# Both halves of the activations side by side, and one 512-column product for the upper weights

## The chip, the cores and the metric

The kernel runs on one core of a Trainium2 chip. The metric is the device time of one execution, in microseconds (us): from the runs below, the median of three. The core has five engines that take their instructions from queues of their own and wait for each other by semaphores: TensorE (PE in the profile, with the loads of its stationary operand as PEld), VectorE (DVE), ScalarE (ACT), GpSimd (POOL) and SyncE (SP), which here only starts transfers.

## What is computed

The reference runs two transformer layers' worth of blocks over 256 tokens of 1024 features, in float32. Cut to what matters here:

```
h    = rms_norm(x)                       # [256, 1024]
proj = h @ w_in                          # 10 blocks of 1024 columns: q, k, v, conv (3), q_m, gates (3)
o    = diff_attention(q, k, v)           # 8 heads, two softmaxes each
conv = gate_b * causal_conv(gate_c * x_c)
x    = x + (g0*(o @ w_attn_o) + g1*(conv @ w_conv_o) + g2*(mem_attn @ w_mem_o)) @ w_o
x    = x + square(relu(h2 @ w_mlp_in)) @ w_mlp_out            # 1024 -> 4096 -> 1024
# second block: mod = silu(c) @ ada_w (adaLN), grouped-query attention + MLP, gated MLP over tokens + MLP
```

Nearly all the work is matrix products of 256 tokens with weights of 1024 rows or more; the weights are read once each.

## The kernel before

**Three products for one.** TensorE multiplies float32r operands, which hold fewer bits than float32. So each operand is split into an upper half, rounded to float32r, and a lower half, the rest. A product is then three: upper by upper, activation's lower by weight's upper, activation's upper by weight's lower, all added up in one PSUM bank. The class `Weights` loads 1 MB of weights at a time (`raw`, three buffers, line 64 on SP's queue) and splits it in two *halves*: the upper part by a cast on ACT (line 86), the lower part by a subtraction on DVE (line 87). It does this in the order of use, six halves ahead of TensorE, into a ring of seven. `W.get` takes the next half, `W.done` says that one is used up and issues the cast for the half six further on and the subtraction for the one before it.

**Three kinds of product loop.** `gemm_cols` (line 407) and `Rows` (505) keep 128 tokens stationary and stream 512 columns of weights through `mm3` (396 to 399). `gemm_feat` (491 to 503) is the other way round: a 128x128 block of weights is stationary and 256 tokens are streamed, so that the result has features on the partitions. One call makes 256 features: for `j` = 0 and 1, one half of weights each, 8 steps `k` with three matmuls of 256 columns (497, 498, 499). Both `j` write one bank `[2, 256]`, and the caller reads the bank when both are done. There are 84 calls: 12 in the gated convolution, 24 in the merging of the three branches, 12 in each of three MLPs, 12 in the gated MLP of the second block.

**Activations.** An activation operand (`hT`, `oT`, `omT`, `cvT`, `mgT`, `memh`, `act`) is a list of two tiles `[128, 8, 256]`, upper and lower. `split_to` (276 to 278) fills them: a cast on ACT, a subtraction on DVE.

**The order of work** is the program's order on each engine, written by hand. `tick()` (378) is called between halves: it runs what is due (`later`), one filler from a list, and now and then a step of the adaLN product (`ada_step`, 1002: ACT starts a transfer, DVE multiplies and adds). In the convolution the fillers are the eight heads of differential attention, four ticks a head and in a software pipeline: `dif_a` (860: scores on PE, mask and maxima on DVE, four exponentials on ACT), then `dif_ot` and `dif_b` (883: DVE mixes the two softmaxes), then `dif_o` and `dif_n`, then `dif_t` (896: PE transposes what `dif_b` wrote, line 900).

**Who reads the banks of gemm_feat.** Convolution (963 to 981): `xc` is copied by ACT; the second product is multiplied by it on DVE (970) and convolved there (974, 976); the third is multiplied on DVE (979) and split. Branches (1045): ACT's sigmoid, and DVE's product. MLP (1142 to 1146): `square` is a Relu and a Square on ACT (1118, 1120), then `split_to`; in each quarter of an MLP four calls are followed by eight halves of `Rows`. Gated MLP (1399): ACT's Gelu.

**PSUM.** Two rings of four banks: `ps_a` (products of most stages, and `dif_t` in the convolution) and `ps_x` (everything else, and `gemm_feat` in the MLPs and the gated MLP). A bank is taken again when its last reader is done.

Of the kernel before, what the change touches and what calls it, by code (L numbers as in the profile page):

```python
# [15 lines left out]
P = 128  # L16
# [6 lines left out]

class Weights:
    """The weights in the order of their use: 1 MB loads, each split in two halves into
    operands hi (rounded to float32r) and lo (the exact rest)."""
# [66 lines left out]
    def first(self, kind, key):  # L93
        """The index of the first half of a load."""
        return 2 * next(i for i, u in enumerate(self.plan) if u[:2] == (kind, key))
# [8 lines left out]
    def done(self, rest=True):  # L104
        """One more half is used up: go on with the loads and splits (lo only up to rest() if told so)."""
        self.used += 1
        self.pump()
        if rest:
            self.rest(self.KEEP)
# [3 lines left out]
def kernel(  # L113
# [28 lines left out]
    # ------------------------------------------------------------------ the weights' order  # L142
# [53 lines left out]
    # ------------------------------------------------------------------ loads at the start  # L196
# [12 lines left out]
    memh = [memin.tile([P, 8, 256], F32R, name=f"memh{i}") for i in range(2)]  # L209
# [50 lines left out]
    # ------------------------------------------------------------------ helpers  # L260
    def rsqrt(ss, inv, y, E=None):
        """y = 1/sqrt(ss*inv + EPS) by Newton's steps from the usual first guess."""
# [26 lines left out]
    def transposed(t, xn, gcol, bcol, dst):  # L289
        """A function that makes dst[hi, lo][:, :, tokens t] = (xn * g + b)^T, xn in two halves."""  # L290
# [38 lines left out]
    def norm(t, src, ssp, gcol, bcol, dst, E=None):  # L329
        """dst[hi, lo][:, :, tokens t] = (src over its root mean square * g + b)^T with g, b per feature;  # L330
        ssp: the sums of squares of src's halves. In three parts: this one, and two to be called later."""
# [32 lines left out]
    def later(n, f):  # L364
        """f runs n ticks on."""
        due.append((clock[0] + n, f))
# [40 lines left out]
    def gemm_cols(key, n0, act, evac, fill=1, acc=None, i0=0):  # L407
        """512 columns: act^T (tokens on partitions out) @ w; evac(the token tiles' psums)."""
# [13 lines left out]
    def gap():  # L422
        """A product that may run while TensorE would wait for operands."""
        if gaps:
            gaps.popleft()()

    def gemm_cols_skew(key, n0s, act, evacs, second, fill=1):
        """The first two of some chunks of columns: the first token tile runs six halves of weights
        ahead, while second() makes the operands of the other."""
# [36 lines left out]
    def gemm_cols_start(key, n0, act, evac, second, fill=1):  # L466
        """The first columns: two halves of weights for a token tile in turn; second() makes the operands
        of the other."""
# [22 lines left out]
    def gemm_feat(key, f0, act, p=ps_a, fill=1):  # L491
        """256 features: w^T @ act (features on partitions out), in one bank [2, 256 tokens]."""
        acc = bank(p).rearrange("p (j c) -> p j c", j=2)
        for j in range(2):
            wh, wl = W.get("B", (key, f0))
            for k in range(8):
                T.matmul(acc[:, j], wh[:, k, :], act[0][:, k, :], start=(k == 0), stop=False)  # L497
                T.matmul(acc[:, j], wh[:, k, :], act[1][:, k, :], start=False, stop=False)  # L498
                T.matmul(acc[:, j], wl[:, k, :], act[0][:, k, :], start=False, stop=(k == 7))  # L499
            W.done()  # L500
            if j == 0:
                tick(fill)
        return acc

    class Rows:
        """out [256, 1024] += act^T @ w by rows of w, in four banks."""
# [13 lines left out]
        def run(self, k0, acts, evac=None, fill=1):  # L520
            """acts: (act pair, index) of rows k0.. in order."""
# [45 lines left out]
    # ------------------------------------------------------------------ small vectors  # L567
# [10 lines left out]
    hT = [const.tile([P, 8, 256], F32R, name=f"hT{i}") for i in range(2)]  # L578
# [91 lines left out]
    # ------------------------------------------------------------------ memory attention  # L670
# [5 lines left out]
    def transpose4(src, dst, on_act=True, scale=None):  # L676
        """dst (a [P, 4, 128] view) = the four [128, 128] blocks of src [P, 512], transposed."""
# [60 lines left out]
    omT = [b1.tile([P, 8, 256], F32R, name=f"omT{i}") for i in range(2)]  # L738
# [10 lines left out]
    def softmax_a(ps, rs, p):  # L749
        """p [P, 2, 256] = exp(rs*(ps - max)) per row and half; returns the sums."""  # L750
# [15 lines left out]
    def transpose_p(p, dst, on_act=True):  # L766
        """p [P q, 2 t, 256 k] -> dst [P k, 2 kb, 256 q]"""
# [35 lines left out]
    def slots(nh, stages):  # L803
        """Software pipeline: per slot, groups of (lag, piece) become one filler each."""
# [6 lines left out]
    # ------------------------------------------------------------------ q, k, v of differential attention  # L811
# [48 lines left out]
    def dif_a(h):  # L860
        """Scores of a head's two components in a bank each: [P, 128 keys] and [P, 256 keys] of the two query tiles."""
# [75 lines left out]
    for n in range(2):  # L937
# [3 lines left out]
        if n == 0:  # L941
# [8 lines left out]
            oT = [oTp.tile([P, 8, 256], F32R, name=f"oT{i}") for i in range(2)]  # L950
# [5 lines left out]
    # ------------------------------------------------------------------ gated convolution  # L956
    convp = pool(right, "conv", side="right")
    cvT = [convp.tile([P, 8, 256], F32R, name=f"cvT{i}") for i in range(2)]
# [4 lines left out]
    for f in range(4):  # L963
        xc = tmp("kn", 2).rearrange("p (j c) -> p j c", j=2)
        ps = gemm_feat("in", XC + 256 * f, hT)
        S.copy(xc, ps)
        tick()
        ps = gemm_feat("in", GC + 256 * f, hT)
# [503 lines left out]
```

## Time and the profile before

| | |
|---|---|
| runs, us | 1336.23, 1336.67, 1340.35 (median 1336.67) |
| span of the profiled execution, us | 1335.7 |
| PE busy | 1315.5 us, 98% of the span, 7883 matmuls |
| PEld busy | 1141.9 us, 85% |
| DVE busy | 926.9 us, 69% |
| ACT busy | 731.2 us, 55% |
| POOL busy | 140.0 us, 10% |
| read from memory | 273 MB, 205 GB/s over the span |

The profile is of one execution, of which it gives the span from the first to the last instruction; no other time is given for that execution. Matmuls are pipelined: the busy time of one matmul (about 0.28 us for 256 columns) is longer than the distance to the start of the next, so what a matmul costs is read from starts in a timeline, and not from the busy column. A busy share is an average over stages.

### The profile page before, as it was taken

What the parts mean: (1) busy time and instruction counts of PE and PEld (TensorE: products, weight loads), DVE (VectorE), ACT (ScalarE), POOL (GpSimd) and SP (SyncE); (2) the same over time, 40 slices, a digit from 0 to 9 for tenths busy, and PEclk for the clock granted to TensorE, in tenths of its full rate; (3) what the DMA queues carried; (4) which work ended last, traced back from release to release, by engine and by line L of the source; (5) the groups of instructions that cost most, each with busy time, mean ns of one, the idle gap of its engine ahead of it and who ended that gap; (6) DMA issues with size and microseconds to landing.
All of it is one profiled execution on the core that took longest, in us unless ns stands there. A gap on an engine that the chain in (4) does not pass through costs nothing.

```text
span 1335.7 us, 20533 instructions
## 1 busy us (share of the span) xinstructions
PE 1315.5 (98%) x7883; PEld 1141.9 (85%) x7883; DVE 926.9 (69%) x1424; ACT 731.2 (55%) x1184; POOL 140.0 (10%) x375
## 2 busy tenths in 40 slices
PE   8899999999999999999899999999999999999998
PEld 6788789999998889987657889987789988799896
DVE  5555678755776778777776787676888877764453
ACT  6765665554444655445575755445646543674451
POOL 1522154500001000100400000000000000000000
PEclk8999999999999999999899999999999999999999
DMA  6572344456885788984313687894886765465650
GB/s 235 201 247 95 127 149 163 154 199 217 269 273 173 237 293 288 285 305 144 110 63 111 200 297 254 269 315 151 292 269 222 253 229 194 135 208 187 214 190 32
DMA packets 166959, 275.43 MB, mean 206 GB/s; under 512 B 8412, under 2 KB 95244, under 8 KB 166732
## 3 DMA queue, kind: packets, MB, share of 16 engines
q1 hardware_dynamic: 137260, 219.78, 48.7%
q10 hardware_dynamic: 27808, 50.41, 11.5%
q0 software_dynamic: 1792, 3.92, 1.1%
q8 instruction: 62, 1.02, 0.3%
q14 instruction: 37, 0.30, 0.1%
HBM read 273.04 MB, written 1.05 MB: 205 GB/s over the span
## 4 chain that ended last, share of the span: by engine, by line
PE 93%; DMA 2%; POOL 1%; DVE 1%; ACT 1%; issue 1%; SPq 0%; ACTq 0%; DVEq 0%; POOLq 0%
PE bank L397 15%; PE bank L399 15%; PE bank L398 15%; PE bank L497 12%; PE bank L499 12%; PE bank L498 12%; PE bank L447 2%; PE bank L1274 1%; PE bank L1254 1%; PE bank L1386 1%; PE bank L438 1%; PE bank L771 1%; PE bank L295 1%; PE bank L680 1%; PE bank L1034 1%
## 5 line engine op out<-in xcount | busy, mean ns | idle before, releaser
L86 ACT CAST whi<-raw 128x1024 fp32r<-128x1024 f32 x412 | 426.3, 1051 | 277.1 <-PE bank L399 79.7
L87 DVE TENSOR_TENSOR wlo<-raw,whi 128x1024 fp32r<-128x1024 f32 x412 | 496.3, 1220 | 90.7 <-ACT whi L86 89.6
L497 PE MATMUL bank<-hT,whi 128*128 128x256 f32 x1152 | 328.6, 285 | 0.0
L499 PE MATMUL bank<-hT,wlo 128*128 128x256 f32 x1152 | 324.8, 282 | 0.0
L498 PE MATMUL bank<-hT,whi 128*128 128x256 f32 x1152 | 324.5, 282 | 0.0
L497 PEld LDWEIGHTS bank<-hT,whi 128*128 128x128 f32 x1152 | 216.5, 188 | 1.9 <-issue 1.3
L498 PEld LDWEIGHTS bank<-hT,whi 128*128 128x128 f32 x1152 | 217.5, 189 | 0.6
L499 PEld LDWEIGHTS bank<-hT,wlo 128*128 128x128 f32 x1152 | 217.1, 188 | 0.0
L397 PE MATMUL bank<-whi,act 128*128 128x512 f32 x384 | 152.2, 396 | 0.0
L398 PE MATMUL bank<-wlo,act 128*128 128x512 f32 x384 | 151.7, 395 | 0.0
L399 PE MATMUL bank<-whi,act 128*128 128x512 f32 x384 | 151.6, 395 | 0.0
L397 PE MATMUL bank<-whi,hT 128*128 128x512 f32 x308 | 128.2, 416 | 0.8 <-ACT hT L321 0.8
L399 PE MATMUL bank<-whi,hT 128*128 128x512 f32 x308 | 122.7, 398 | 0.0
L398 PE MATMUL bank<-wlo,hT 128*128 128x512 f32 x308 | 122.5, 398 | 0.0
L1018 DVE SCALAR_TENSOR_TENSOR acc<-araw,cond,acc 128x512 f32<-128x512 f32 x128 | 95.6, 747 | 27.4 <-DMA araw<-in_ada_w_dram 27.0
L399 PEld LDWEIGHTS bank<-whi,act 128*128 128x128 f32 x384 | 72.0, 187 | 17.5
L397 PEld LDWEIGHTS bank<-whi,act 128*128 128x128 f32 x384 | 72.0, 187 | 17.0
L398 PEld LDWEIGHTS bank<-wlo,act 128*128 128x128 f32 x384 | 72.0, 188 | 16.9
L397 PEld LDWEIGHTS bank<-whi,hT 128*128 128x128 f32 x308 | 58.3, 189 | 18.8 <-ACT hT L321 4.2
L399 PEld LDWEIGHTS bank<-whi,hT 128*128 128x128 f32 x308 | 58.4, 190 | 15.1 <-DVE hT L310 1.0
L398 PEld LDWEIGHTS bank<-wlo,hT 128*128 128x128 f32 x308 | 58.5, 190 | 13.5 <-issue 0.7
L278 DVE TENSOR_TENSOR act<-s,act 128x512 fp32r<-128x512 f32 x36 | 24.9, 691 | 58.2 <-ACT act L277 58.2
(298 smaller groups left out, 1893.9 us busy)
## 6 DMA issues: line engine op xcount, KB each, us to landing
araw<-in_ada_w_dram ACTq DMA_DIRECT2D x192, 256.0 KB
raw<-in_w_in_dram SPq DMA_DIRECT2D x40, 1024.0 KB
raw<-in_mlp_w_in_dram SPq DMA_DIRECT2D x32, 1024.0 KB
raw<-in_mlp_w_out_dram SPq DMA_DIRECT2D x32, 1024.0 KB
raw<-in_gmlp_w_in_dram SPq DMA_DIRECT2D x24, 1024.0 KB
raw<-in_w_mlp_in_dram SPq DMA_DIRECT2D x16, 1024.0 KB
raw<-in_w_mlp_out_dram SPq DMA_DIRECT2D x16, 1024.0 KB
raw<-in_gmlp_w_out_dram SPq DMA_DIRECT2D x12, 1024.0 KB
```

Of the source, the lines that this page charges most:

```text
L86: self.nc.scalar.copy(hv, v)
L87: self.rests.append(lambda v=v, hv=hv, lv=lv: self.nc.vector.tensor_sub(lv, v, hv.bitcast(F32)))
L278: V.tensor_sub(lo, src, hi.bitcast(F32))
L295: T.transpose(pss[g][:, j * P:(j + 1) * P], xn[g][:, j * P:(j + 1) * P], ident)
L397: T.matmul(acc, xh, wh, start=start, stop=False)
L398: T.matmul(acc, xh, wl, start=False, stop=False)
L399: T.matmul(acc, xl, wh, start=False, stop=stop)
L447: T.matmul(acc[c][0], act[e][:, k, 0:P], w[0][:, j, :], start=(k + e == 0), stop=False)
L497: T.matmul(acc[:, j], wh[:, k, :], act[0][:, k, :], start=(k == 0), stop=False)
L498: T.matmul(acc[:, j], wh[:, k, :], act[1][:, k, :], start=False, stop=False)
L499: T.matmul(acc[:, j], wl[:, k, :], act[0][:, k, :], start=False, stop=(k == 7))
L1018: V.scalar_tensor_tensor(acc, ada_st.pop(j), cond[:, k:k + 1], acc, op0=ALU.mult, op1=ALU.add)
```

## The change

An operand becomes one tile `[128, 8, 2, 256]`, in which upper and lower half of the same step `k` lie side by side; a small class `Pair` gives the two halves as views, and the 512 columns of a step as `both(k)`. In `gemm_feat` the upper weights multiply those 512 columns in one matmul into a full bank, `acc[:, 0]` for the upper and `acc[:, 1]` for the lower half; the lower weights multiply the upper half as before, into `acc[:, 1]`. Each `j` has a bank of its own. After each `j`, ACT copies `acc[:, 1]` to a tile in SBUF, and DVE adds `acc[:, 0]` to it. Callers read that tile. It is taken from the two-buffer scratch rings `kn` and `hf`.

```diff
+class Pair:
+    def __init__(self, tile):
+        self.tile = tile
+    def __getitem__(self, e):
+        return self.tile[:, :, e, :]
+    def both(self, k):
+        return self.tile[:, k]
...
+    def operand(p, name, **kw):
+        return Pair(p.tile([P, 8, 2, 256], F32R, name=name, **kw))
...
-    hT = [const.tile([P, 8, 256], F32R, name=f"hT{i}") for i in range(2)]
+    hT = operand(const, "hT")
...
-    def gemm_feat(key, f0, act, p=ps_a, fill=1):
-        acc = bank(p).rearrange("p (j c) -> p j c", j=2)
+    def gemm_feat(key, f0, act, dst, p=ps_a, fill=1):
         for j in range(2):
+            acc = bank(p).rearrange("p (e c) -> p e c", e=2)
             wh, wl = W.get("B", (key, f0))
             for k in range(8):
-                T.matmul(acc[:, j], wh[:, k, :], act[0][:, k, :], start=(k == 0), stop=False)
-                T.matmul(acc[:, j], wh[:, k, :], act[1][:, k, :], start=False, stop=False)
-                T.matmul(acc[:, j], wl[:, k, :], act[0][:, k, :], start=False, stop=(k == 7))
+                T.matmul(acc, wh[:, k, :], act.both(k), start=(k == 0), stop=False)
+                T.matmul(acc[:, 1], wl[:, k, :], act[0][:, k, :], start=False, stop=(k == 7))
             W.done()
+            S.copy(dst[:, j], acc[:, 1])
+            V.tensor_add(dst[:, j], acc[:, 0], dst[:, j])
             if j == 0:
                 tick(fill)
-        return acc
+        return dst
...
-        ps = gemm_feat("in", XC + 256 * f, hT)
-        S.copy(xc, ps)
+        gemm_feat("in", XC + 256 * f, hT, xc)
...
-        ps = gemm_feat("in", GC + 256 * f, hT)
+        ps = gemm_feat("in", GC + 256 * f, hT, tmp("kn", 2).rearrange("p (j c) -> p j c", j=2))
...
-        ps = gemm_feat("in", goff + 256 * f, hT)
+        gemm_feat("in", goff + 256 * f, hT, sg)
         for j in range(2):
-            S.activation(sg[:, j], ps[:, j], AF.Sigmoid, bias=c1("bg", 8 * bi + 2 * f + j))
+            S.activation(sg[:, j], sg[:, j], AF.Sigmoid, bias=c1("bg", 8 * bi + 2 * f + j))
...
-                    ps = gemm_feat(ki, 1024 * q + 256 * f, hT, p=ps_x)
-                    s_ = square(ps.rearrange("p j c -> p (j c)")).rearrange("p (j c) -> p j c", j=2)
+                    ps = tmp("hf", 2)
+                    gemm_feat(ki, 1024 * q + 256 * f, hT, ps.rearrange("p (j c) -> p j c", j=2), p=ps_x)
+                    s_ = square(ps).rearrange("p (j c) -> p j c", j=2)
```

The other operands and callers are changed in the same way.

## Rows read from the trace of the kernel before

**Rows 1.** Page: span; busy us of the engines; shares of the chain of waits.
```profile
span 1335.7 us, 20533 instructions
PE 1315.5 (98%) x7883; PEld 1141.9 (85%) x7883; DVE 926.9 (69%) x1424; ACT 731.2 (55%) x1184; POOL 140.0 (10%) x375
PE 93%; DMA 2%; POOL 1%; DVE 1%; ACT 1%; issue 1%; SPq 0%; ACTq 0%; DVEq 0%; POOLq 0%
PE bank L397 15%; PE bank L399 15%; PE bank L398 15%; PE bank L497 12%; PE bank L499 12%; PE bank L498 12%; PE bank L447 2%; PE bank L1274 1%; PE bank L1254 1%; PE bank L1386 1%; PE bank L438 1%; PE bank L771 1%; PE bank L295 1%; PE bank L680 1%; PE bank L1034 1%
```

**Rows 2.** Groups by line, gemm_feat's first product: shapes, count | busy us, mean ns | idle.
```profile
L497 PE MATMUL bank<-hT,whi 128*128 128x256 f32 x1152 | 328.6, 285 | 0.0
...
L497 PE MATMUL bank<-omT,whi 128*128 128x256 f32 x64 | 18.2, 284 | 0.0
L497 PE MATMUL bank<-oT,whi 128*128 128x256 f32 x64 | 18.2, 284 | 0.0
...
L497 PE MATMUL bank<-cvT,whi 128*128 128x256 f32 x64 | 18.0, 281 | 0.0
```

**Rows 3.** Timeline of PE in the first MLP: start us, busy us, what.
```profile
470.23 0.28 PE L497 MATMUL bank<-hT,whi 128*128 128x256 f32 x1
...
475.99 0.28 PE L497 MATMUL bank<-hT,whi 128*128 128x256 f32 x1
...
476.35 0.39 PE L397 MATMUL bank<-whi,act 128*128 128x512 f32 x1
...
488.95 0.39 PE L397 MATMUL bank<-whi,act 128*128 128x512 f32 x1
...
498.51 0.39 PE L399 MATMUL bank<-whi,act 128*128 128x512 f32 x1
498.74 0.28 PE L497 MATMUL bank<-hT,whi 128*128 128x256 f32 x1
```

**Rows 4.** Groups by line and shape: a copy and a subtraction that read 256 columns of a bank.
```profile
L916 ACT COPY on<-bank 128x256 f32<-128x256 f32 x8 | 3.0, 373 | 0.3
L278 DVE TENSOR_TENSOR oT<-bank,oT 128x256 fp32r<-128x256 f32 x8 | 3.4, 420 | 5.8 <-ACT oT L277 5.8
```

**Rows 5.** Windows: stretch, length, busy PE, PEld, DVE, ACT, POOL; clock, DMA share, GB/s.
```profile
200.00:220.00 20.00, 20.00 (x168) 19.06 (x168) 17.42 (x38) 10.79 (x30) 8.51 (x21) 1.00 0.53 180
450.00:475.00 25.00, 25.00 (x203) 24.55 (x202) 21.32 (x26) 19.72 (x28) 0.00 (x0) 1.00 0.85 281
475.00:500.00 25.00, 25.00 (x120) 20.61 (x119) 17.06 (x20) 10.19 (x12) 0.00 (x0) 1.00 0.93 300
```

**Rows 6.** Timeline of ACT, one head's slot in the convolution; in brackets idle before.
```profile
205.40 0.46 ACT L879 ACTIVATE p<-bank,bias,rsd 128x128 f32<-128x128 f32 x1 [5.98 <-DVE bias L876]
...
207.37 1.05 ACT L86 CAST whi<-raw 128x1024 fp32r<-128x1024 f32 x1
```

**Rows 7.** Timeline of DVE, that slot and the end of the next head's.
```profile
206.42 0.69 DVE L979 TENSOR_TENSOR hf<-bank,hf 128x512 f32<-128x512 f32 x1
208.97 0.69 DVE L278 TENSOR_TENSOR cvT<-hf,cvT 128x512 fp32r<-128x512 f32 x1 [1.86 <-ACT cvT L277]
...
210.37 0.75 DVE L890 SCALAR_TENSOR_TENSOR p<-p,cc 128x128 f32<-128x128 f32 x2
...
222.97 0.75 DVE L890 SCALAR_TENSOR_TENSOR p<-p,cc 128x128 f32<-128x128 f32 x2
```

**Rows 8.** Timeline of PE: the transposes that read what L890 wrote.
```profile
211.24 0.49 PE L900 MATMUL bank<-ident,p 128*128 128x128 f32 x3
...
225.02 0.49 PE L900 MATMUL bank<-ident,p 128*128 128x128 f32 x3
```

**Rows 9.** Timeline of ACT, one call of gemm_feat in the first MLP: its Relu.
```profile
466.83 0.59 ACT L1118 ACTIVATE kn<-bank 128x512 f32<-128x512 f32 x1
```

**Rows 10.** Timeline of DVE, the same call: its lower half.
```profile
468.78 0.69 DVE L278 TENSOR_TENSOR act<-s,act 128x512 fp32r<-128x512 f32 x1 [0.27 <-ACT act L277]
```

More of the change, by code (lines that the diff above doesn't have):

```diff
@@ L21, with __iter__ @@
 RSQRT_SEED = 0x5F3759DF
+class Pair:
[3 more added lines that the diff above has]
+        return self.tile[:, :, e, :]
+    def __iter__(self):
+        return iter((self[0], self[1]))
+    def both(self, k):
+        return self.tile[:, k]
 class Weights:
@@ L208 @@
     memin = pool(memin_st, "memin", side="right")
-    memh = [memin.tile([P, 8, 256], F32R, name=f"memh{i}") for i in range(2)]
+    memh = operand(memin, "memh")
     mt = [memin.tile([P, D], F32, name=f"mt{t}") for t in range(NT)]
@@ L737 @@
     b1 = pool(left, "b1")
-    omT = [b1.tile([P, 8, 256], F32R, name=f"omT{i}") for i in range(2)]
+    omT = operand(b1, "omT")
     qkv_st = ExitStack()
@@ L949 @@
             oTp = pool(right, "oTp", side="right")
-            oT = [oTp.tile([P, 8, 256], F32R, name=f"oT{i}") for i in range(2)]
+            oT = operand(oTp, "oT")
             kq_p[0] = pool(kq_st, "kq2", side="right")
@@ L957 @@
     convp = pool(right, "conv", side="right")
-    cvT = [convp.tile([P, 8, 256], F32R, name=f"cvT{i}") for i in range(2)]
+    cvT = operand(convp, "cvT")
     inner_st = ExitStack()
@@ L977 @@
         tick()
-        ps = gemm_feat("in", GB + 256 * f, hT)
+        ps = gemm_feat("in", GB + 256 * f, hT, tmp("kn", 2).rearrange("p (j c) -> p j c", j=2))
         V.tensor_tensor(y, ps, y, op=ALU.mult)
@@ L1046, in branch @@
         sg = tmp("kn", 2).rearrange("p (j c) -> p j c", j=2)
-        ps = gemm_feat("in", goff + 256 * f, hT)
+        gemm_feat("in", goff + 256 * f, hT, sg)
         for j in range(2):
-            S.activation(sg[:, j], ps[:, j], AF.Sigmoid, bias=c1("bg", 8 * bi + 2 * f + j))
+            S.activation(sg[:, j], sg[:, j], AF.Sigmoid, bias=c1("bg", 8 * bi + 2 * f + j))
         tick()
-        ps = gemm_feat(key, 256 * f, act)
+        ps = gemm_feat(key, 256 * f, act, tmp("hf", 2).rearrange("p (j c) -> p j c", j=2))
         if f not in accs:
@@ L1073 @@
             mgp = pool(right, "mgT", side="right")
-            mgT = [mgp.tile([P, 8, 256], F32R, name=f"mgT{i}") for i in range(2)]
+            mgT = operand(mgp, "mgT")
             for j in range(3):
@@ L1112, in mlp @@
         acts = {}
-        act0 = [actp.tile([P, 8, 256], F32R, tag=f"act{i}", name=f"act{i}", bufs=2) for i in range(2)]
+        act0 = operand(actp, "act", tag="act", bufs=2)
         acts[0] = act0
@@ L1140, in mlp @@
             if q < 4:
-                act = [actp.tile([P, 8, 256], F32R, tag=f"act{i}", name=f"act{i}", bufs=2) for i in range(2)]
+                act = operand(actp, "act", tag="act", bufs=2)
                 for f in range(4):
-                    ps = gemm_feat(ki, 1024 * q + 256 * f, hT, p=ps_x)
-                    s_ = square(ps.rearrange("p j c -> p (j c)")).rearrange("p (j c) -> p j c", j=2)
+                    ps = tmp("hf", 2)
+                    gemm_feat(ki, 1024 * q + 256 * f, hT, ps.rearrange("p (j c) -> p j c", j=2), p=ps_x)
+                    s_ = square(ps).rearrange("p (j c) -> p j c", j=2)
                     split_to(act[0][:, 2 * f:2 * f + 2, :], act[1][:, 2 * f:2 * f + 2, :], s_)
@@ L1398 @@
         if i < 12:
-            ps = gemm_feat("gin", 256 * i, hT, p=ps_x)
+            ps = gemm_feat("gin", 256 * i, hT, tmp("kn", 2).rearrange("p (j c) -> p j c", j=2), p=ps_x)
             u = prodp.tile([P, 2, 256], F32, tag="u", name="u", bufs=2)
```

## The prediction

> **What bounds the kernel now.** I read the chain of waits first, and there the shares by engine: TensorE holds 93% of the span of 1335.7 us, the lines of gemm_feat 36% (497 to 499) and those of mm3 45% (396 to 399) [rows 1]. The order of matmuls is all that ends late; DVE and ACT are busy 926.9 and 731.2 us beside it [rows 1]. In the windows of the stages concerned PE has no gap at all, at a granted clock of 1.00, which is 2.4 GHz, the upper level [rows 5]. So a shorter stream of matmuls shortens the kernel by as much, as long as DVE and ACT still deliver in time. The windows say how much room they have, and it is little where it matters: DVE is busy 17.42 of 20 us in the convolution, and 21.32 of 25 us during the gemm_feat calls of the first MLP [rows 5].
>
> **The change on TensorE.** The groups by line give the count: line 497 runs 1152 + 3 x 64 = 1344 times [rows 2], once for each step k of the 84 calls. The busy time there (about 285 ns) is not its price, as matmuls overlap; the timeline's starts are. From 470.23 to 475.99 us lie 48 matmuls of 256 columns: 120.0 ns each. From 476.35 to 488.95 lie 54 of 512: 233.3 ns each. Going from one width to the other costs nothing extra: the last three of 256 take 0.36 us up to the first of 512, and the last of 512 takes 0.23 us up to the first of 256 [rows 3]. A step is 3 x 120.0 = 360.0 ns before, and 233.3 + 120.0 = 353.3 ns after. That is 6.7 ns x 1344 = 9.0 us less, though a third of the matmuls are gone: 768 columns go through as before, and only what a matmul costs beside its columns is saved. Bounds: no row has the two widths in turn, so at worst the saving is 0; at best all 768 columns run at the rate of the wide one (350 ns), 13.4 us. I take 9.0, each width at its own row.
>
> The Trainium skill ("TensorE: Matmul & The Clock Gate", Back-to-back issue gap) gives N / 2.4 + 2.5 ns from start to start, so 2.5 ns for each matmul saved. By that the sum would begin with 3.4 us instead. This trace disagrees with both of its values (109.2 ns against 120.0 here, 215.8 against 233.3), and the rows decide.
>
> **What is added.** Per half of weights (168 of them) a copy of 256 columns on ACT and an addition of 256 on DVE. The nearest rows are a copy from a bank, 373 ns, and a subtraction with a bank as source, 420 ns [rows 4]: 63 us more on ACT and 71 us more on DVE, against 605 and 409 us in which they now do nothing. In sum that is free. In place it is not, as both work in program order. Before, nothing read the bank after j = 0, and after j = 1 ACT or DVE read it once. Now, after every half, ACT waits for PE, then DVE waits for ACT; in the MLP, ACT then waits for DVE (Relu), and DVE again for ACT (the cast ahead of the lower half). Queued behind the copy are the weight casts, the exponentials and the transfers of adaLN; behind the addition the lower parts of the weights, the convolution and dif_b. PE waits for those.
>
> *Convolution.* Look at one head's slot. ACT idles 5.98 us for the maxima, runs its exponentials from 205.40 and the next weight cast at 207.37 [rows 6]. DVE's product of the third convolution input starts at 206.42, then it idles 1.86 us for a cast on ACT, and the last mix of dif_b starts at 210.37 and takes 0.75 [rows 7]: it is done at 211.12. PE's transposes of it start at 211.24 [rows 8]. The room is 0.1 us. Now three additions come ahead of the maxima in this slot, less a little that was idle: 1.0 us. So the exponentials end at 208.4, the cast at 209.3, the copy of the half at 209.7; the addition, which must follow that copy, ends at 210.1; then come the product at 206.42 before, the cast, two lower halves and dif_b, 3.4 us: 213.5. PE waits 2.4 us. In the next head's slot dif_b is done at 223.72 and read at 225.02 [rows 7, 8], a room of 1.3; the addition now stands behind exponentials and cast in the same way, and DVE carries its lateness over, since it has no idle to lose (17.42 of 20 us, and 7 additions of 0.42 make 20.4 [rows 4, 5]). I take 2.4 us again, and for the two heads after it, as DVE drains, 1.4 together: 6.2 us. Bounds: 0, if the room of later heads swallows it, and 4 x 2.4 = 9.6.
>
> *MLPs.* In a call of two halves DVE is busy 21.32 / 25 x 5.76 = 4.9 us [rows 5]. Relu to lower half takes 468.78 - 466.83 = 1.95 us on ACT [rows 9, 10]; DVE does other work meanwhile and idles 0.27 of it [rows 10]. Now the addition stands directly before the Relu and the lower half directly after the cast, with nothing between in DVE's queue: it idles those 1.95 us. So 4.9 + 0.84 + 1.95 = 7.7 us a call, where PE takes 16 x 0.3533 = 5.65: DVE falls 2.0 us behind a call, 8 us in the four calls of a quarter. The eight halves of Rows behind them last 8 x 12 x 0.2333 = 22.4 us, in which DVE is idle 7.94 of 25 [rows 5], so 7.1 us are won back. A ring of four banks with one bank a half lets an addition be three halves late, 8.5 us; weights are split six halves ahead. So PE hardly sees it, but for the first calls, where the transposes of the act tiles take two of the four banks: 1 us. The second and third MLP have a lower rate of adaLN steps or none: 0.5 us each. In all 2.0, between 0 and the 10.7 of the rival below.
>
> *The rest.* Branches and gated MLP: the same additions, with the reader of the sum next on the same DVE queue or a Gelu on ACT that DVE doesn't wait for. Cost 0 on PE, hidden by three halves of bank reach; up to 1 us if not. Pair tiles: the same elements in two runs of 256 columns; sigmoid, Relu and Gelu read SBUF instead of a bank. Both lie beside PE; where DVE is short they belong to the bounds above. The copy of xc by ACT was there before and becomes part of the new one.
>
> **Sum.** -9.0 + 6.2 + 2.0 = -0.8 us on a span of 1335.7. The runs' median is 1.0 us above that span, which I leave: 1336.67 - 0.8 = 1335.9, so **1336 us**.
>
> **The rivals.**
> *Everything stays hidden.* DVE's lateness is swallowed by the heads' room and the banks; PE gives back 1 us of 9: 1336.67 - 8.0 = 1328.7. For it: PE has no wait in these stages now, and three of the four heads I looked at have over a microsecond of room. Against: the slot with 0.1 us [rows 7, 8], and DVE at 87% before anything is added [rows 5].
> *DVE is not paid back in the first MLP (slower).* In the Rows stretch the transfers are already at 0.93 of the DMA engines [rows 5]. DVE can only catch up on weights that have arrived; with 7% of 22.4 us, 1.6 us a quarter are won back instead of 7.1, and 6.4 are carried on: 19.2 after three quarters. From 8.5 us on, the reach of the banks, PE stands: 10.7 us. -9.0 + 6.2 + 10.7 + 1.0 = +8.9: 1345.6. Against: three raw buffers fill while DVE is slow in the calls, so the catching up starts from full buffers.
> *The change doesn't do what it says.* Wide and narrow in turn take 360 ns a step, because a narrow matmul between two wide ones takes 127 ns; the saving is 0 and the waits stay: +8.2, 1344.9. Against: the two changes of width in rows 3. By the skill's page on TensorE named above, 3.4 us are saved, and it would be 1341.5; its values miss both rows.
>
> **Chances.** Forecast 0.46, with a range of its own from 1331 to 1340; hidden 0.23; DVE not paid back 0.17; no saving 0.14. What a measurement of this kernel can tell from no change is about 0.3%, 4 us. Faster by more: 0.21 of the hidden case and 0.07 of the forecast, 0.28. Slower by more: 0.16 of the DVE case, 0.10 of the last, 0.02 of the forecast, 0.28. Within: 0.44. The range reaches to the hidden case and over the slower ones' times: 1328.5 to 1347.
>
> **What would show it.** In the changed kernel's timeline: a step of 353 ns in an undisturbed stretch of gemm_feat (right), 360 (the last rival). Waits of PE at line 900's transposes for dif_b on DVE between 180 and 260 us, some 6 us, and DVE over 95% busy there; if PE has none, the convolution step is wrong. In the first MLP an idle of nearly 2 us on DVE before each lower half of act, and waits of PE for banks of about 1 us; 10 us mean the DVE rival. I'd be wrong altogether if PE waited for weights, or if the time moved by over 4 us with PE's waits as before.

## The result, and the profile after

The changed kernel takes 1359.19 us (median of 4 runs, 1358.18 to 1360.85), beside 1337.82 us for the kernel before on the same chip: a ratio of 1.016, 95% interval 1.0147 to 1.0172 (intervals below are of the same kind). It is 21.4 us slower. The forecast was 1336, the range ended at 1347.

First the page of the changed kernel: the span, the engines, and the chain that ended last, by engine and by line [rows 1].

```profile
span 1357.0 us, 17998 instructions
PE 1317.9 (97%) x6539; PEld 1073.9 (79%) x6539; DVE 983.4 (72%) x1592; ACT 782.0 (58%) x1348; POOL 141.5 (10%) x375
...
PE 70%; DVE 14%; DMA 6%; ACT 5%; issue 2%; POOL 2%; SPq 0%; ACTq 0%; DVEq 0%; POOLq 0%
PE bank L518 15%; PE bank L417 12%; PE bank L418 12%; PE bank L419 12%; PE bank L519 8%; DVE wlo L103 5%; DMA araw<-in_ada_w_dram 4%; PE bank L467 2%; DVE acc L1039 2%; PE bank L1296 1%; PE bank L1276 1%; DVE gate L1039 1%; PE bank L1408 1%
```

TensorE held 93% of the chain before; now it holds 70%. The rest went to DVE, to the transfers of the adaLN weights (araw) and to ACT. So the kernel stopped being bound by TensorE alone. TensorE's products themselves got what was promised and more. Its timeline in an undisturbed stretch, from the first step of a call to a step 36 steps on (line 518 is the wide product, 519 the narrow one) [rows 3]:

```profile
505.01 0.39 PE L518 MATMUL bank<-hT,whi 128*128 128x512 f32 x1
505.24 0.28 PE L519 MATMUL bank<-hT,wlo 128*128 128x256 f32 x1
505.36 0.39 PE L518 MATMUL bank<-hT,whi 128*128 128x512 f32 x1
...
517.61 0.39 PE L518 MATMUL bank<-hT,whi 128*128 128x512 f32 x1
```

12.60 us for 36 steps is 350.0 ns a step, against 360.0 before: 10.0 ns x 1344 steps, 13.4 us.

To see where the time went, I cut all traces at the same matmuls: the first that reads q, the first of the branch on cvT, the first output product after the branches, and the first product of the loop that opens each later stage (line 447 before, 467 after); the third MLP is counted to the end. Lengths in us, each column from one profiled execution; later columns are experiments told below.

| stage | before | after | wide, no sum | copy only | add only | late split | mlp1 old | ada resident | araw5 | late, conv old | late select |
|---|---|---|---|---|---|---|---|---|---|---|---|
| attention, convolution, first gate | 125.5 | 133.9 | 124.5 | 127.8 | 129.3 | 134.5 | 134.6 | 134.5 | 133.9 | 125.3 | 125.3 |
| branches | 133.0 | 130.0 | 130.0 | 130.0 | 130.0 | 130.1 | 129.9 | 130.1 | 130.0 | 130.0 | 130.1 |
| first MLP | 187.4 | 204.1 | 185.5 | 185.5 | 206.2 | 191.2 | 187.4 | 187.4 | 195.9 | 196.0 | 187.4 |
| second MLP | 188.4 | 187.7 | 186.5 | 186.5 | 188.0 | 187.2 | 188.1 | 187.8 | 188.7 | 187.1 | 187.0 |
| gated MLP | 226.3 | 225.0 | 224.5 | 224.5 | 224.7 | 224.9 | 224.9 | 224.9 | 225.0 | 225.0 | 225.0 |
| third MLP | 190.4 | 188.6 | 188.5 | 188.5 | 188.5 | 188.5 | 188.7 | 188.8 | 188.5 | 188.9 | 188.5 |

The loss sits in two stages: 8.4 us in the first row, 16.7 in the first MLP. The other four gain 6.8 together; the rest (start and the stretches between) loses 3.0, which gives the 21.3 us between the spans. Of these 3.0, 1.6 lie between the first and the second MLP, a stretch without gemm_feat, which takes 115.0 to 118.1 us in the executions of this table.

**The convolution.** TensorE's waits there (us in total, times, longest), of which the kernel before has none:

```profile
PE bank L922 <- DVE p L912: 4.6, 2, 2.5
PE bank L954 <- DVE on L947: 2.1, 2, 1.4
```

One head's slot, first on ACT, then on DVE, then on TensorE (start, length, engine, line; in brackets the idle before) [rows 6 to 8], and the window around it [rows 5]:

```profile
209.09 1.05 ACT L102 CAST whi<-raw 128x1024 fp32r<-128x1024 f32 x1
210.02 0.39 ACT L521 COPY kn<-bank 128x256 f32<-128x256 f32 x1
```
```profile
210.44 0.42 DVE L522 TENSOR_TENSOR kn<-bank,kn 128x256 f32<-128x256 f32 x1 [2.22 <-ACT kn L521]
...
213.68 0.75 DVE L912 SCALAR_TENSOR_TENSOR p<-p,cc 128x128 f32<-128x128 f32 x2
```
```profile
214.18 0.74 PE L922 MATMUL bank<-ident,p 128*128 128x128 f32 x3 [2.51 <-DVE p L912]
```
```profile
200.00:220.00 20.00, 17.49 (x107) 14.23 (x106) 16.64 (x36) 9.78 (x25) 8.73 (x18) 1.00 0.43 140
```

The copy stands on ACT behind exponentials and the weight cast; DVE idles 2.22 us for it, everything behind the addition is late, and the transposes of dif_b wait 2.51 us. The next head's slot shows the same wait with 2.10 us. DVE is busy 16.64 of 20 us here, less than the 17.42 before: it is late because it waits, and not because it is full.

**The first MLP.** DVE around two lower halves (line 298), and ACT between them [rows 9, 10]:

```profile
483.42 0.42 DVE L522 TENSOR_TENSOR hf<-bank,hf 128x256 f32<-128x256 f32 x1
485.85 0.69 DVE L298 TENSOR_TENSOR act<-s,act 128x512 fp32r<-128x512 f32 x1 [2.01 <-ACT act L297]
486.46 0.75 DVE L1039 SCALAR_TENSOR_TENSOR gate<-araw,cond,gate 128x512 f32<-128x512 f32 x1
...
493.61 0.69 DVE L298 TENSOR_TENSOR act<-s,act 128x512 fp32r<-128x512 f32 x1 [2.02 <-ACT act L297]
...
502.88 0.75 DVE L1039 SCALAR_TENSOR_TENSOR gate<-araw,cond,gate 128x512 f32<-128x512 f32 x1 [1.39 <-DMA araw<-in_ada_w_dram]
...
517.44 0.75 DVE L1039 SCALAR_TENSOR_TENSOR acc<-araw,cond,acc 128x512 f32<-128x512 f32 x1 [1.90 <-DMA araw<-in_ada_w_dram]
```
```profile
483.87 0.63 ACT L1139 ACTIVATE kn<-hf 128x512 f32<-128x512 f32 x1 [1.90 <-DVE hf L522]
484.53 0.63 ACT L1141 ACTIVATE s<-kn 128x512 f32<-128x512 f32 x1
485.19 0.62 ACT L297 CAST act<-s 128x512 fp32r<-128x512 f32 x1
```

Addition on DVE; Relu, Square and cast on ACT; lower half on DVE: a trip to the other engine and back, for which DVE stands 2.0 us in each call. The adaLN step that follows at 486.46 needs nothing of it, yet waits its turn. The Trainium skill says that ACT and DVE take their queues strictly in order ("TensorE: Matmul & The Clock Gate", Architectural detail: the array is 16x 32x32, not 1x 128x128); that pair of lines agrees. The two lower halves lie 7.76 us apart (485.85 to 493.61), which is what this call takes on DVE.

Windows of the changed kernel (stretch, length, busy time of PE, PEld, DVE, ACT, POOL, the granted clock, DMA share, GB/s). The first two go by DVE, which runs behind TensorE: up to 494.3 it works on the calls of a quarter, then up to 514.5, its next addition, on what is queued for the Rows halves. TensorE runs those Rows halves from 482.6 to 505.0. The last two are stretches with waits of TensorE [rows 5].

```profile
475.00:500.00 25.00, 25.00 (x120) 20.62 (x119) 18.92 (x26) 15.06 (x22) 0.00 (x0) 1.00 0.74 227
500.00:520.00 20.00, 19.46 (x104) 16.37 (x103) 14.72 (x18) 7.07 (x10) 0.00 (x0) 1.00 0.99 354
...
520.00:530.00 10.00, 6.76 (x31) 5.45 (x31) 6.32 (x10) 7.21 (x12) 1.01 (x2) 0.86 0.63 192
...
620.00:630.00 10.00, 7.88 (x25) 5.34 (x24) 6.83 (x10) 3.50 (x6) 0.00 (x0) 0.83 0.86 277
```

Before, the DMA engines were busy 0.85 of the time in the window of the calls and 0.93 in that of the Rows halves [rows 5]. Now it is 0.74 and 0.99 (0.93 from 494.3 to 514.5): fewer transfers run while DVE is slow in the calls, and from 500 to 520, where it should catch up, DVE idles 5.28 of 20 us, most of it for adaLN tiles.

How late DVE is can be read from its additions. Here are TensorE's last matmul and DVE's addition of the last half of the first quarter, and of the first half of the second; first in the changed kernel, then in ada_resident, an experiment told below in which adaLN tiles are always at hand.

```profile
482.50 0.28 PE L519 MATMUL bank<-hT,wlo 128*128 128x256 f32 x1
491.17 0.42 DVE L522 TENSOR_TENSOR hf<-bank,hf 128x256 f32<-128x256 f32 x1
507.69 0.28 PE L519 MATMUL bank<-hT,wlo 128*128 128x256 f32 x1
514.46 0.42 DVE L522 TENSOR_TENSOR hf<-bank,hf 128x256 f32<-128x256 f32 x1
```
```profile
482.11 0.28 PE L519 MATMUL bank<-hT,wlo 128*128 128x256 f32 x1
490.69 0.42 DVE L522 TENSOR_TENSOR hf<-bank,hf 128x256 f32<-128x256 f32 x1
507.31 0.28 PE L519 MATMUL bank<-hT,wlo 128*128 128x256 f32 x1
510.58 0.42 DVE L522 TENSOR_TENSOR hf<-bank,hf 128x256 f32<-128x256 f32 x1
```

Behind the end of TensorE's half, the addition is 8.4 us late at the end of the quarter and 6.5 at the start of the next: 1.9 us are won back in the Rows halves. In ada_resident it is 8.3 and 3.0, so 5.3 are won back, which leaves no more than the first addition of the stage has (3.0 us in the changed kernel, 3.6 in this one).

TensorE's waits in this stage (the last, for hT, is there before too):

```profile
PE bank L518 <- DVE hf L522: 4.0, 5, 1.5
PE bank L418 <- DVE wlo L103: 3.7, 3, 1.8
PE bank L1055 <- DVE hf L522: 2.8, 2, 1.8
PE bank L417 <- ACT hT L341: 0.8, 1, 0.8
```

That is 10.5 us. On top, the granted clock falls in stretches with such waits: windows of 10 us in this stage have 0.86 (from 520), 0.97 (530), 0.83 (570) and 0.83 (620) as the mean of the two levels, 2.4 and 1.2 GHz, where before all are at 1.00. The missing shares add up to 1.4 + 0.3 + 1.7 + 1.7 = 5.1 us. Waits, clock, less 1.9 us saved (192 steps x 10 ns) make 13.7 of the 16.7. The other 3 us are for the most part in how a wait is counted: its idle begins at the modelled end of the matmul before it, some 0.16 us after the next matmul would have started. From start to start in the two timelines the ten waits take 12.3 us, the lower clock beside them 4.6 and many short delays 1.4; less the saving, that is the 16.7. In the convolution the same count gives 7.4 us of waits (6.7 by the idle shown), 1.7 of clock (0.83 from 230 to 240) and 1.1 of short delays, less some 2 saved (208 steps): the 8.4.

### The profile page after: what moved, and what is told of

The parts are those of the page before. It is cut to its first block, busy times and chain, and to the rows that moved or that the text cites. A ratio compares the mean times of both kernels' runs of the same rounds, so it can differ in the third digit from the quotient of the medians.

```text
span 1357.0 us, 17998 instructions
## 1 busy us (share of the span) xinstructions
PE 1317.9 (97%) x6539; PEld 1073.9 (79%) x6539; DVE 983.4 (72%) x1592; ACT 782.0 (58%) x1348; POOL 141.5 (10%) x375
## 4 chain that ended last, share of the span: by engine, by line
PE 70%; DVE 14%; DMA 6%; ACT 5%; issue 2%; POOL 2%; SPq 0%; ACTq 0%; DVEq 0%; POOLq 0%
PE bank L518 15%; PE bank L417 12%; PE bank L418 12%; PE bank L419 12%; PE bank L519 8%; DVE wlo L103 5%; DMA araw<-in_ada_w_dram 4%; PE bank L467 2%; DVE acc L1039 2%; PE bank L1296 1%; PE bank L1276 1%; DVE gate L1039 1%; PE bank L1408 1%; PE bank L793 1%; PE bank L315 1%
## 5 line engine op out<-in xcount | busy, mean ns | idle before, releaser
L102 ACT CAST whi<-raw 128x1024 fp32r<-128x1024 f32 x412 | 426.8, 1051 | 186.5 <-PE bank L419 47.7
L518 PE MATMUL bank<-hT,whi 128*128 128x512 f32 x1152 | 414.8, 400 | 4.6 <-DVE hf L522 4.3
L518 PEld LDWEIGHTS bank<-hT,whi 128*128 128x128 f32 x1152 | 218.3, 189 | 58.6 <-DVE hf L522 6.0
L522 DVE TENSOR_TENSOR hf<-bank,hf 128x256 f32<-128x256 f32 x96 | 40.3, 420 | 26.4 <-ACT hf L521 26.1
L1039 DVE SCALAR_TENSOR_TENSOR gate<-araw,cond,gate 128x512 f32<-128x512 f32 x64 | 47.8, 746 | 11.1 <-DMA araw<-in_ada_w_dram 11.0
```

The costliest lines, as they stand in the source:

```text
L102: self.nc.scalar.copy(hv, v)
L518: T.matmul(acc, wh[:, k, :], act.both(k), start=(k == 0), stop=False)
L522: V.tensor_add(dst[:, j], acc[:, 0], dst[:, j])
L1039: V.scalar_tensor_tensor(acc, ada_st.pop(j), cond[:, k:k + 1], acc, op0=ALU.mult, op1=ALU.add)
```

## The experiments

Each is the changed kernel with the edit that is told, cut to its main lines; a `...` marks lines left out. Times are set against the kernel before on the same chip.

**Is the wide product good by itself?** This kernel (the kernel without sums, below) leaves out copy and addition, and with them part of the sums; readers take the second half of the bank.

```diff
-            S.copy(dst[:, j], acc[:, 1])
-            V.tensor_add(dst[:, j], acc[:, 0], dst[:, j])
...
-        return dst
+        return acc
...
```

> The wide product alone: the copy and the addition after each half are left out, and the readers read the second half's bank as they read it before (the first half's bank is not read), so part of the sums is left out. Theory A (the wide product saves 10 ns at each of 1344 steps, as the changed kernel's timeline shows where nothing disturbs it, and all the loss comes from the evacuation in order): 1337.8 - 13.4 = 1324, no new waits of PE. Rival B (the wide product itself costs, by weights that are used up sooner than they arrive or by a lower clock): above 1335, with PE waits in the first MLP as in the changed kernel.

1326.59 us, ratio 0.991 (0.989 to 0.9929), 11.6 us below the kernel before. The product pays: 1.9 us in each MLP, which is 192 x 10 ns. Everything lost comes with the summing of the halves.

**And the other way round: narrow products, with copy and addition.**

```diff
-                T.matmul(acc, wh[:, k, :], act.both(k), start=(k == 0), stop=False)
+                if k == 0:
+                    T.matmul(acc, wh[:, k, :], act.both(k), start=True, stop=False)
+                else:
+                    for e in range(2):
+                        T.matmul(acc[:, e], wh[:, k, :], act[e][:, k, :], start=False, stop=False)
```

> The evacuation alone: three products of 256 columns as before (only step 0 of each half wide), into a bank for each half, and the copy and the addition after each half. Theory A: the waits come from the evacuation, so they stay, and 7 of 8 steps are 10 ns longer: 1359.2 + up to 11.8 where nothing waits, some less where PE waits anyway: 1366 to 1371. Rival B (the wide product is at fault): near the kernel before, 1338 to 1342.

1369.25 us, 1.023 (1.0213 to 1.0246): 10.1 us above the changed kernel, for 7 of 8 steps made narrow again (1176 x 10 ns = 11.8). Together with the run before, this parts the change into a gain of some 11 us and a cost of some 33.

**Does it matter which engine copies?**

```diff
-            S.copy(dst[:, j], acc[:, 1])
+            V.tensor_copy(dst[:, j], acc[:, 1])
```

> The changed kernel, with the copy after each half on DVE instead of ACT, just ahead of the addition. Theory A1 (in the convolution the addition is late because the copy stands behind dif_a's exponentials on ACT): the convolution's loss, 8.4 us from its start to the first product of cvT, falls to 2 to 4 us although DVE has 168 more copies; the first MLP still loses, as DVE still stands still during Relu, Square and cast: 16 to 22 us there. Rival A2 (DVE simply has too much to do): the convolution loses more, 12 to 18 us, and the first MLP over 22.

1397.07 us, 1.0439 (1.0412 to 1.0467); first MLP 214.0, convolution 138.4. With both on DVE there is no wait for ACT ahead of the addition, but all stages up to and with the gated MLP are longer than in the changed kernel: DVE's load counts, and the theory that only the order of copy and addition costs falls.

**The trip to ACT and back in the MLPs: cast and lower half issued two weight steps later.**

```diff
-                    split_to(act[0][:, 2 * f:2 * f + 2, :], act[1][:, 2 * f:2 * f + 2, :], s_)
+                    later(2, lambda act=act, f=f, s_=s_: split_to(act[0][:, 2 * f:2 * f + 2, :], act[1][:, 2 * f:2 * f + 2, :], s_))
```

> The changed kernel, with the cast and the lower half of each MLP activation issued two ticks (a call) later, so that DVE's lower half no longer stands right behind the addition while ACT runs Relu, Square and cast. Theory A3 (those 2.0 us of idle per call, 24 us in the first MLP, put DVE behind): the first MLP's loss of 16.7 us falls below 5, total near 1345. Rival A4 (DVE is late there because the adaLN steps wait for transfers that ACT issues late, or because raw weights come late): the loss falls by under 4 us, total above 1355.

1344.8 us, 1.0045 (1.003 to 1.006). The first MLP loses 3.8 us instead of 16.7, with the same additions. DVE's waits of over 6 us there, first of the changed kernel, then of this one:

```profile
DVE act L298 <- ACT act L297: 25.6, 14, 2.0
DVE acc L1039 <- DMA araw<-in_ada_w_dram: 9.4, 7, 2.0
DVE gate L1039 <- DMA araw<-in_ada_w_dram: 7.5, 4, 2.7
```
```profile
DVE acc L1039 <- DMA araw<-in_ada_w_dram: 12.3, 7, 4.6
DVE gate L1039 <- DMA araw<-in_ada_w_dram: 6.5, 5, 2.3
DVE act L298 <- ACT act L297: 6.5, 6, 1.8
```

The place of two instructions of a call, the cast in ACT's queue and the lower half in DVE's, is worth 14.4 us of the 21.4.

**The convolution taken apart.** copy_only leaves out the addition (readers take the copy):

```diff
-            V.tensor_add(dst[:, j], acc[:, 0], dst[:, j])
```

> The changed kernel with the addition on VectorE left out (ScalarE's copy of the second half of the bank stays and is what all readers read; a part of the sums is left out). Two theories of the convolution's loss (8.4 us over the kernel before, 9.4 over the kernel that only has the wide products): by the first, 'order', it is the addition that stands behind the copy, which stands behind exponentials and cast, so without the addition PE has no wait of over 1 us at dif_b's transposes and the stage from the first q product to the first v product lasts 124.5 to 126.5 us; by the second, 'ScalarE', it is the copy itself that delays the exponentials and the casts behind it, and the stage lasts 129 or more. First MLP (187.4 before, 204.1 changed): without the addition nothing ties VectorE to the end of a product, so 186 to 190 if the round trip of addition, Relu, cast, lower half is the cause, 195 or more if ScalarE's copy is. Time 1327 to 1333 by the first of each, 1340 or more by the second.

1329.59 us (one run). The stage lasts 127.8, between the two theories. add_only leaves out the copy, and the addition takes a tile of x instead:

```diff
-            S.copy(dst[:, j], acc[:, 1])
-            V.tensor_add(dst[:, j], acc[:, 0], dst[:, j])
+            V.tensor_add(dst[:, j], acc[:, 0], xt[0][:, 0:256])
```

> The changed kernel without ScalarE's copy: the addition takes, beside the first half of the bank, a tile that is there from the start (the second half of the bank is left out of the sums). VectorE has the same number of instructions of the same size as in the changed kernel, but its addition waits for TensorE alone. Convolution (125.5 us before, 133.9 changed): 'order' (the addition waits for a copy that stands behind exponentials and cast) says 125 to 128; 'load' (three additions of 0.42 us a slot on an engine that is busy 17.4 of 20 us) says 131 or more. First MLP: the Relu on ScalarE still waits for the addition and the lower half for the cast behind it, so by the round-trip theory the idle of about 2 us before each lower half stays and the stage lasts 198 to 205; by a theory that ScalarE's copy is what makes the round trip long, 190 to 195.

1354.23 us (one run); the stage lasts 129.3, again between. TensorE's waits in the convolution, of copy_only and then of add_only:

```profile
PE bank L921 <- DVE p L911: 1.7, 2, 0.9
PE bank L953 <- DVE on L946: 1.0, 1, 1.0
```
```profile
PE bank L953 <- DVE on L946: 2.1, 2, 1.4
PE bank L921 <- DVE p L911: 1.0, 2, 0.6
```

From 124.5 without either, the copy alone costs 3.3, the addition alone 4.8, both 9.4. So neither theory holds by itself: the copy has about a third and the addition a half. The 1.3 left, for the addition having to follow the copy, are little to build on: five executions with the same code in this stage last 133.9 to 134.6. In the first MLP the answer is clear, though each run is a single one: 185.5 with the copy alone, as without either, and 206.2 with the addition alone (expected were 198 to 205). There the copy costs nothing; the addition ahead of the Relu is all of it.

**Why is it not paid back? No adaLN transfers.** The weights of adaLN are transferred for the first three tiles, and these are used for all later steps (so the modulation is made from other weights); all instructions of DVE and ACT stay.

```diff
+            if j < 3:
+                t = ada_p[0].tile([P, 512], F32, name=f"araw{j}")
...
+                ada_keep.append(t)
+            ada_st[j] = ada_keep[j % 3]
...
```

> The changed kernel, with the weights of adaLN transferred for the first three tiles only and these used again for all later steps (the modulation is computed from wrong weights; every VectorE and ScalarE instruction stays). In the first MLP of the changed kernel VectorE idles 25.6 us before the lower halves and 16.9 us for tiles of adaLN weights. Theory 'transfers' (the lateness of a call can't be won back in the Rows stretch, since its transfers, late themselves, fill the DMA engines there): without them the idle of 25.6 us stays, the waits for adaLN tiles go, VectorE catches up in each quarter, and the stage lasts 186 to 193 us where the changed kernel has 204.1 (187.4 before). Theory 'idle alone' (12 calls x 2.0 us, and nothing else, is more than VectorE can make up in any case): 199 or more. Elsewhere the transfers of adaLN end after the first MLP or matter little, so the convolution stays at 132 to 135.

1339.39 us (one run); the first MLP 187.4, to the tenth what it lasts before. DVE's longest wait in the stage, and the window of the Rows halves:

```profile
DVE act L298 <- ACT act L297: 25.9, 14, 2.0
```
```profile
500.00:520.00 20.00, 20.00 (x109) 17.11 (x108) 17.95 (x23) 10.87 (x15) 0.00 (x0) 1.00 0.67 216
```

The idle of 2.0 us a call is all still there, and it costs next to nothing (the kernel without sums has 185.5), since DVE, with tiles always at hand, is busy 17.95 us there instead of 14.72 and catches up. One thing this run doesn't part: without transfers ACT doesn't stand for free adaLN buffers either, for which it waits 51.8 us in this stage of the changed kernel (44.5 before).

**Ring or DMA engines? Five adaLN buffers instead of three in the first MLP.**

```diff
+            if deep[0] and j % 5 > 2:
+                t = deep[1].tile([P, 512], F32, tag="araw2", name="araw2", bufs=2)
...
+        while j and deep[2] <= j + (4 if deep[0] else 2):
+            ada_load(deep[2])
...
```

> The changed kernel with two more buffers for adaLN tiles during the first MLP (five instead of three), nothing left out. If the lateness isn't won back because three buffers and a transfer of some 5 us are too short a ring (VectorE finds no tile, though the DMA engines could deliver), the stage goes from 204.1 to 190-198 and the time to 1345-1353, ratio 1.005 to 1.011. If the DMA engines themselves are full in the Rows stretch (share 0.94 to 1.06 there in the changed kernel), more buffers move the waiting only: 200 to 205, ratio 1.013 to 1.018.

1352.05 us, 1.0101 (1.0085 to 1.0117): 7.2 of the 21.4 us are back. In the profiled execution the stage lasts 195.9. Its window from 500 to 520, and the longest waits of ACT and of TensorE in the stage:

```profile
500.00:520.00 20.00, 20.00 (x105) 16.87 (x104) 17.11 (x21) 8.50 (x11) 0.00 (x0) 1.00 1.02 361
```
```profile
ACT whi L102 <- DMA raw<-in_w_mlp_in_dram: 22.1, 6, 6.3
```
```profile
PE bank L518 <- DVE hf L522: 7.4, 5, 1.8
```

DVE no longer waits for adaLN tiles, but the DMA engines are now full (1.02), and the weights themselves come late (9.4 us of waits for them in the changed kernel). So the ring was too short, as the stage's time in the range of the ring theory says, and behind it the transfers are. How much each has is not shown: the profiled execution is the fastest of its four (1348.79), and the granted clock stays at 1.00 in this stage, where the lower level took up to 5 of the 16.7 us in the changed kernel. TensorE's waits fall only from 10.5 to 7.9.

**Is the MLP's loss its own?** Narrow products in the first MLP alone.

```diff
+                    if ki in ("m1i",):
+                        ps = gemm_feat_old(ki, 1024 * q + 256 * f, hT, None, p=ps_x).rearrange("p j c -> p (j c)")
...
```

> The changed kernel with the three narrow products back in the first MLP alone (no copy, no addition, no late split there). If the first MLP's loss is its own, the stage is at 187 to 189 as before and the time at 1341 to 1344, ratio 1.002 to 1.005. If part of it is lateness that comes out of the convolution, whose loss of 8.4 us is still there, the stage is at 192 or more and the time at 1347 or more.

1342.79 us, 1.0036 (1.0023 to 1.0048), the stage 187.4: the lateness of the convolution (134.6 in this execution) does not reach it.

**Versions that keep what pays.** late_conv_old is late_split with narrow products in the convolution and the first gate:

```diff
-        gemm_feat("in", XC + 256 * f, hT, xc)
+        S.copy(xc, gemm_feat_old("in", XC + 256 * f, hT, xc))
...
```

> The changed kernel with the three narrow products back in the convolution and the first gate (no addition there), and the split of an MLP activation issued two weight steps later as in late_split. From late_split (1344.8): the convolution's stage goes from 134.5 to 125.5 or 126, the rest stays, the first MLP at 191: 1335 to 1336.5, ratio to the kernel before 0.998 to 0.999. If the lateness that comes out of the convolution is what the first MLP's or the branches' times rest on, these move too: branches 131 to 133, and the time is 1338 to 1340.

1337.89 us, 0.9991 (0.9977 to 1.0005). The convolution is back at 125.3, but the first MLP now takes 196.0 where late_split has 191.2, and single runs lie between 1331.88 and 1341.34. The sum of parts was 2 us too low here: that stage swings, with 6.7 us of waits of TensorE in this execution and 3.2 in that of late_split. With five adaLN buffers added:

> late_conv_old with two more buffers for adaLN tiles during the first MLP, as in araw5. In late_conv_old that stage still lasts 196.0 us against 187.4 before, though VectorE's idle before the lower halves is down from 25.6 to 7.0 us; it waits 22.4 us for adaLN tiles. Theory 'ring': what is left is lateness that three buffers can't make up, so with five the stage lasts 186 to 189 us and the time is 1328 to 1331, ratio 0.992 to 0.995. Theory 'load' (the 24 additions of 0.42 us are too much for VectorE in any case): 193 or more, ratio 0.997 or more.

1333.06 us, 0.9958 (0.9945 to 0.9972), the stage 188.6 as the ring theory had it; the whole ended 2 us above its 1328 to 1331. Instead of the buffers, late_select has narrow products in the first MLP too:

> As late_conv_old, and the first MLP with the three narrow products too: the wide product only in the branches, the second and third MLP and the gated MLP, where the stages of the changed kernel were 3.0, 0.7, 1.8 and 1.3 us shorter than before. If stages are independent: 1337.8 - 7 = 1331, ratio 0.994 to 0.996. If the gain of these stages was lateness handed from stage to stage (a wait that would have come there had been paid earlier), the ratio is 0.998 or more.

1331.69 us, 0.9947 (0.9931 to 0.9963): faster than both kernels, by 6.5 us than the one before. Its shares of the chain, by engine:

```profile
PE 89%; DVE 3%; DMA 3%; ACT 2%; POOL 1%; issue 1%; SPq 0%; ACTq 0%; DVEq 0%; POOLq 0%
```

The same without the late split:

> As late_select (three narrow products in the convolution and in the first MLP, the wide product everywhere else), with the split of an MLP activation at its old place. If the late split matters only where DVE has nothing to spare, that is in the first MLP with the addition, this is the same as late_select: 1331 to 1333, ratio 0.994 to 0.996. If the round trip of addition, Relu, cast and lower half costs in the second and third MLP too, it is 1334 to 1338, and these stages last 189 or more instead of 187.0 and 188.5.

1333.36 us, 0.9966 (0.9954 to 0.9978). The second MLP lasts 189.2 instead of 187.0, the third 188.5 in both; the intervals overlap, so what the late split is worth there stays open.

## Why the prediction was wrong

*The TensorE step* was right in kind and too low by a third: 350.0 ns a step, not 353.3, so 13.4 us and not 9.0. The wide and the narrow one in turn reach what stood as the upper bound. Worked out from the isolated gaps that the Trainium skill gives ("TensorE: Matmul & The Clock Gate", Back-to-back issue gap), a step would be an estimated 3 x 109.17 = 327.5 ns before and 215.8 + 109.2 = 325.0 after; the traces have neither of these steps, nor the 2.5 ns between them.

*The convolution step* named the mechanism and the place: the addition behind the copy behind exponentials and cast, and 2.4 us twice at the transposes, measured 2.51 and 2.10. Its last term, 1.4 us for two more heads, stands against 2.1 us at line 954, where other transposes wait, for dif_n. So 6.2 us of waits were predicted and 6.7 came; with the saving added back the stage lost some 10.5, as it also has the lower clock (1.7) and delays too short to be seen as waits. The sign that was named beside it failed: DVE over 95% busy. It is at 83% (16.64 of 20 us), so the reason given for lateness being carried over, a DVE with no idle to lose, does not hold there. The runs add that the order of copy and addition alone has little of it (1.3 of 9.4): copy and addition cost 3.3 and 4.8 each by itself.

*The MLP step failed.* Its first half was right: DVE idles 1.95 us a call (2.01), and a call takes it 7.7 us (7.76 in the lines above, 7.0 to 9.0 in others). The sentence that failed is that the Rows halves "last 8 x 12 x 0.2333 = 22.4 us, in which DVE is idle 7.94 of 25 [rows 5], so 7.1 us are won back". That idle was read as room. It was in large part DVE waiting for adaLN tiles, in the whole stage of the kernel before:

```profile
DVE acc L1018 <- DMA araw<-in_ada_w_dram: 18.3, 10, 3.3
DVE gate L1018 <- DMA araw<-in_ada_w_dram: 11.5, 9, 2.8
```

Only part of that idle could be turned into work: these waits fall from 29.8 to 16.9 us, by 12.9, where three times 7.1 had been counted on. Behind the first quarter 1.9 us were won back and not 7.1; behind the second none (the additions are 6.9 us late at its end, 8.9 at the start of the third). ada_resident shows that the transfers are what stands in the way: when the tiles are at hand, the whole 16.7 us go away with the 2.0 us a call still in place. Whether it is more DVE's wait for a tile or ACT's wait for a free buffer, no run parts. I took 1 us for this stage; it cost 16.7, and 18.6 without the saving.

*The rival "DVE is not paid back in the first MLP"* had this mechanism, and 10.7 us for it; I gave it 0.17. I put it down to full DMA engines alone, and argued against it that "three raw buffers fill while DVE is slow in the calls". The raw weights of this product indeed came no later than before (ACT waits 9.4 us for them, 11.8 before); it is the adaLN tiles that DVE waits for. The DMA share in the calls fell from 0.85 to 0.74, and that work was left for a stretch that had been nearly full already (0.93). TensorE's waits of 10.5 us are close to its 10.7, in part by chance, as it had 19.2 us of lateness less the reach of the banks. What it lacked in this stage is the lower clock, up to 5.1 us.

*The rest at nothing* held for branches and gated MLP, which gain 3.0 and 1.3 us. In the second and third MLP I took 0.5 us each; against the kernel without sums they lose 1.2 and 0.1.

## What to carry to other kernels

An idle share is room only if the engine could have worked in it: look at what ended the idle, and where that is a transfer, count on a part of it at most (here 12.9 of 29.8 us). An operation that ties two in-order queues together costs its round trip in whatever stands behind it, so cost it as the wait and not as its 0.42 us; issuing the dependent instructions two weight steps later was worth more here (14.4 us) than the wide product (13.4). And take such a change stage by stage: the same edit won 3.0 us in one stage and lost 16.7 in another.

## What the runs showed of the hardware

Alternating matmuls of 512 and 256 columns go at 350.0 ns a pair, faster than the two widths in rows of their own (233.3 + 120.0); the kernel without sums shows the same, as 1.9 us over 192 steps.

In the changed kernel's first MLP the granted clock fell to 0.83 to 0.86 as the mean of 10 us, so to the lower level for some of it, in stretches where TensorE had waited only 0.5 to 1.8 us at a time: 0.54 us before 519.71, 1.77 before 524.55 and 1.47 before 526.68 in one such stretch. Over the whole execution the missing shares from 140 us on add up to 15.3 us, against 6.8 before. The Trainium skill tells of short idles between groups of matmuls that take the clock back ("TensorE: Matmul & The Clock Gate", A second HAM failure mode: psum-queue depth-cycling); these rows agree with it. But waits like these don't always take the clock: araw5 has the same two waits in the convolution, 2.50 and 2.10 us, and 7.4 us in five waits in the first MLP, and its granted clock is 1.00 throughout both stages. Its convolution lasts 133.9 us all the same, with a third wait at those transposes (0.75 us). So the 5.1 us on 10.5 of waits are what one execution showed, and no price of a wait.
